# One weight stream for delta-rule inputs, queries and keys in a two-block fp32 transformer kernel, with weight units split one ahead and the modulation sums on VectorE alone

## The chip, the cores and the metric

The kernel runs on one core of a Trainium2 chip. Its metric is device time in microseconds, the median of several runs. TensorE (PE) multiplies matrices into PSUM; VectorE (DVE), ScalarE (ACT) and GpSimd (POOL) do elementwise work; SyncE (SP) here only issues DMAs. Each engine executes its own instructions in order and waits on semaphores for the others.

## The reference, cut to what matters

Two transformer blocks are applied to 256 tokens of width 2048. The first block modulates its normed input by six vectors of `c` (`w_ada`, 2048 x 12288, is the "modulation" weight), runs a latent attention (queries by `w_uq`, keys and values by `w_ukv`) beside a gated delta rule (`w_in`'s q, k, v columns pass a short convolution first), mixes both and ends with a gated feed-forward. The second has a convolution beside a windowed attention and a squared-ReLU feed-forward.

```python
mod = c_act @ w_ada[l] + b_ada[l]
sh_a, sc_a, gt_a, sh_f, sc_f, gt_f = [m[:, None, :] for m in jnp.split(mod, 6, axis=-1)]
h = _rmsnorm(x, norm_mix[l]) * (1.0 + sc_a) + sh_a
p = h @ w_in[l]
c_q, c_kv, k_pe, q_g, k_g, v_g, z, b_logit, a_logit, gate_logits = _split_cols(p)
y_a = _mla_branch(c_q, c_kv, k_pe, q_a_norm[l], kv_a_norm[l], w_uq[l], w_ukv[l], cos, sin) @ w_o_mla[l]
qkv = jnp.concatenate([q_g, k_g, v_g], axis=-1)
y_b = _gdn_branch(qkv, z, b_logit, a_logit, conv_w[l], A_log[l], dt_bias[l], gdn_norm[l]) @ w_o_gdn[l]
g_a, g_b = jnp.split(jax.nn.sigmoid(gate_logits), 2, axis=-1)
mix = (g_a * y_a + g_b * y_b) @ w_o[l]
x = x + gt_a * mix
h = _rmsnorm(x, norm_ffn[l]) * (1.0 + sc_f) + sh_f
gate, up = jnp.split(h @ w_gate_up[l], 2, axis=-1)
x = x + gt_f * ((jax.nn.silu(gate) * up) @ w_down[l])
...
def _gdn_branch(qkv, z, b_logit, a_logit, conv_w, A_log, dt_bias, gdn_norm):
    ...
    beta = jax.nn.sigmoid(b_logit.astype(jnp.float32))
    g = -jnp.exp(A_log.astype(jnp.float32)) * jax.nn.softplus(a_logit.astype(jnp.float32) + dt_bias.astype(jnp.float32))
    o = _gated_delta_chunked(q, k, v, beta, g)
```

## The kernel before

Activations lie with features on the 128 partitions and the 256 tokens along the free axis. All weights are fp32. A `Stream` reads one weight array in **units** of 128 x 1024 elements (512 KB): SP loads a unit into one of six `raw` buffers, ACT writes its rounded part `hi` (L268), DVE the remainder `lo` (L269), each into one of three buffers, and PE uses both: `mm2` (L302, L303, L305) takes a 512-column product with `hi` and a 256-column one with `lo` for each of a unit's eight blocks. So a unit costs 16 such products on PE, one ACTIVATE and one TENSOR_TENSOR. `Stream.next` hands out the blocks; when a unit is used up and none is ready it loads and splits the next one.

The stages: a first projection `wk` (96 units) with modulation vectors that PE makes itself (`ada_pe`, L426); one small product `misc`, from which the gates of the delta rule follow by a chain of small operations; then four head pairs, in which `pair_in` (convolved q, k, v by `wq`), `queries` (by `wuq` and `wuk`), `pair_mid` and `pair_out` (the delta rule) and `attend` are generators that `merge` steps in order of their costs; `wab` (output projections), `wo`, the first feed-forward (`wgu` and `wdn` in turn, three groups), the second block's `wag`, `wv2`, `wqk`, `wo2`, and its feed-forward (`wup` and `wdn2` in turn, four groups).

Beside these runs a list of fillers: at each new unit `pump` adds `rate[0]` to a credit, and each whole credit makes one step of the first filler. Twelve groups of modulation chunks (`ada_vec`, eight units each, L433 to L447) are such fillers up to `wo`, four more stand in the first feed-forward. A step of `ada_vec` loads one unit into a `raw` buffer; ACT multiplies its first half by a scalar (L440), DVE adds the second half times a scalar (L441), and POOL adds the result to the sum (L443). When a group ends, `ada_fin` (L451, L455) sums it over the partitions on PE.

A scheduler fixes each engine's order when the program is built: an instruction that was emitted earlier goes first among those that its model takes to be ready. The lines are those of the kernel before.

Of the kernel before, what the change touches and what calls it, by code (L numbers as in the profile page):

```python
# [10 lines left out]
AF = mybir.ActivationFunctionType  # L11
# [3 lines left out]
P = 128  # L15
T = 256
D = 2048
# [64 lines left out]
def layout(I):  # L82
# [34 lines left out]
    parts = [wi[:, 1024:1088], wi[:, 5184:5200], np.zeros((D, 48), np.float32)]  # L117
    for h in range(NH):
        for b in (1088, 2112, 3136):
            parts.append(wi[:, b + 128 * h:b + 128 * h + 128])  # L120
    A["wq"] = _blocks(np.concatenate(parts, 1), [(k, c) for c in range(25) for k in range(KT)])
    uq = I["w_uq"][0].reshape(512, 8, 192)
    parts = []
    for h in range(0, 8, 2):
        parts += [uq[:, h, 128:], uq[:, h + 1, 128:], uq[:, h, :128], uq[:, h + 1, :128]]
    A["wuq"] = _blocks(np.concatenate(parts, 1), [(k, c) for c in range(12) for k in range(4)])
    ukv = I["w_ukv"][0].reshape(512, 8, 2, 128)
    A["wuk"] = _blocks(ukv[:, :, 0].reshape(512, 1024), [(k, c) for c in range(8) for k in range(4)])
# [27 lines left out]
def emit(nc, tc, st, a):  # L156
# [87 lines left out]
    class Stream:  # L244
# [168 lines left out]
    def ada_pe(stream, chunks):  # L413
# [3 lines left out]
        for k in range(0, KT, 4):  # L417
            if k:
                yield
            w = []  # L420
            for g in range(4):
                if n * g % stream.size == 0:
                    w.append(stream.unit())
# [68 lines left out]
    def ada_group(ks):  # L492
# [4 lines left out]
        else:  # L497
            for k in ks[::2]:
                yield from ada_pe(ada0, [16 + k, 17 + k, k, k + 1])
# [4 lines left out]
    warm = ps("ps")  # L504
    for i in range(20):
        PE.matmul(warm[:, :P], ones, ones, start=True, stop=True)
# [12 lines left out]
    for gi, ks in enumerate(KGROUPS):  # L519
        drain()  # L520
# [3 lines left out]
        if gi + 1 < len(KGROUPS):  # L524
            nx = KGROUPS[gi + 1]
            filler.append(ada_group(nx))
# [809 lines left out]
```

## Time and profile before

| | |
|---|---|
| median of 3 runs | 2780.33 us (2779.88 to 2781.22) |
| the profiled execution: time, span | 2776.44 us, 2774.7 us |
| PE, weight loads, DVE, ACT, POOL busy | 96%, 82%, 70%, 50%, 13% of the span |
| HBM read | 563.07 MB, 205 GB/s with the writes |

The span runs from the first to the last instruction; the profiled time is 1.7 us longer. A busy PE isn't PE at its peak, so the stages are judged against the two feed-forwards, where PE never idles. PEclk is the granted clock: 1.00 is 2.4 GHz, 0.50 is 1.2 GHz.

### The profile page before, as it was taken

The page shows a single profiled execution, that of the slowest core. Times are in us where ns is not written, and L with a number is a line of the kernel's source. Part 1 is how long each engine was busy: PE and PEld are TensorE (multiplying, and loading weights), DVE is VectorE, ACT ScalarE, POOL GpSimd, SP SyncE. Part 2 cuts the span into 40 slices and gives each one's busy share as a digit, 9 for nine tenths or more (in the row PEclk, how much of TensorE's full clock was granted, in tenths as well). Part 3 has the DMA queues.
Part 4 walks back from the last instruction along what each step waited for, and adds up shares of the span by engine and source line. Part 5 has one row for each costly group of instructions (what it writes and reads, how often), then busy time and mean ns, then how long its engine had stood idle before and what let it go on. Part 6 is the DMA issues. An engine that isn't in the chain of part 4 may idle for free.

```text
span 2774.7 us, 42925 instructions
## 1 busy us (share of the span) xinstructions
PE 2677.4 (96%) x16226; PEld 2275.6 (82%) x16226; DVE 1941.0 (70%) x3066; ACT 1379.0 (50%) x2218; POOL 361.1 (13%) x310
## 2 busy tenths in 40 slices
PE   8999989899989999999999999999989999999997
PEld 5667867777777888888888889888978888888886
DVE  4865687778787877666666689796776566665665
ACT  5334565556554655344434564456554444453453
POOL 0000032223243122000000040000450000000012
PEclk9999989999999999999999999999999999999999
DMA  8795765548787687555555555544545555555553
GB/s 307 275 348 194 256 218 189 170 143 276 268 285 259 212 274 265 189 189 186 190 188 189 189 183 183 190 153 136 184 136 190 190 188 190 187 189 190 189 190 122
DMA packets 171279, 572.19 MB, mean 206 GB/s; under 512 B 19008, under 2 KB 19264, under 8 KB 171072
## 3 DMA queue, kind: packets, MB, share of 16 engines
q1 hardware_dynamic: 164736, 557.92, 59.5%
q10 hardware_dynamic: 6336, 11.53, 1.2%
q8 instruction: 128, 2.10, 0.3%
q14 instruction: 79, 0.65, 0.1%
HBM read 563.07 MB, written 6.29 MB: 205 GB/s over the span
## 4 chain that ended last, share of the span: by engine, by line
PE 78%; DVE 8%; DMA 5%; ACT 3%; issue 3%; POOL 2%; SPq 0%; ACTq 0%; DVEq 0%; POOLq 0%
PE ps L303 17%; PE ps L302 17%; PE ps L305 17%; PE ps L324 4%; PE ps L325 4%; PE ps L326 4%; PE ps L291 3%; PE ps L289 3%; PE ps L290 3%; DVE lo L269 3%; DMA raw<-ada 3%; PE O L426 1%; ACT hi L268 1%; DMA raw<-adaf 1%; DVE raw L441 1%
## 5 line engine op out<-in xcount | busy, mean ns | idle before, releaser
L269 DVE TENSOR_TENSOR lo<-raw,hi 128x1024 fp32r<-128x1024 f32 x856 | 1086.3, 1270 | 453.0 <-ACT hi L268 438.9
L268 ACT ACTIVATE hi<-raw 128x1024 fp32r<-128x1024 f32 x856 | 904.6, 1057 | 787.7 <-PE ps L305 442.1
L303 PEld LDWEIGHTS ps<-H,lo 128*128 128x128 f32 x2816 | 531.2, 189 | 139.2 <-DVE lo L269 21.8
L303 PE MATMUL ps<-H,lo 128*128 128x256 f32 x2816 | 576.5, 281 | 13.1 <-DVE lo L269 12.7
L302 PE MATMUL ps<-H,hi 128*128 128x512 f32 x1408 | 561.9, 400 | 15.5 <-DVE H L340 7.2
L305 PE MATMUL ps<-H,hi 128*128 128x512 f32 x1408 | 557.6, 397 | 0.1
L303 PEld LDWEIGHTS ps<-G,lo 128*128 128x128 f32 x1968 | 369.1, 188 | 92.1 <-DVE lo L269 7.1
L303 PE MATMUL ps<-G,lo 128*128 128x256 f32 x1968 | 389.7, 279 | 5.1 <-DVE lo L269 5.1
L305 PE MATMUL ps<-G,hi 128*128 128x512 f32 x984 | 388.7, 396 | 0.0
L302 PE MATMUL ps<-G,hi 128*128 128x512 f32 x984 | 386.9, 396 | 0.4 <-DVE Y L1056 0.4
L302 PEld LDWEIGHTS ps<-H,hi 128*128 128x128 f32 x1408 | 269.0, 191 | 22.7 <-DVE H L340 8.2
L377 POOL TENSOR_TENSOR acc<-acc,th 128x256 f32<-128x256 f32 x90 | 106.9, 1195 | 1318.4 <-ACT th L380 1317.4
L443 POOL TENSOR_TENSOR ada<-ada,raw 128x512 f32<-128x512 f32 x112 | 182.0, 1625 | 720.9 <-DVE raw L441 601.8
L305 PEld LDWEIGHTS ps<-H,hi 128*128 128x128 f32 x1408 | 265.7, 189 | 2.9 <-DVE H L340 0.3
L302 PEld LDWEIGHTS ps<-G,hi 128*128 128x128 f32 x984 | 187.0, 190 | 1.7 <-issue 0.7
L305 PEld LDWEIGHTS ps<-G,hi 128*128 128x128 f32 x984 | 184.8, 188 | 1.0
L324 PE MATMUL ps<-hi,H 128*128 128x512 f32 x448 | 175.7, 401 | 3.5 <-ACT hi L268 2.9
L325 PE MATMUL ps<-lo,H 128*128 128x512 f32 x448 | 177.0, 395 | 1.1 <-DVE lo L269 1.1
L326 PE MATMUL ps<-hi,H 128*128 128x512 f32 x448 | 175.8, 392 | 0.0
L289 PE MATMUL ps<-H,hi 128*128 128x256 f32 x528 | 151.5, 287 | 0.0
L291 PE MATMUL ps<-H,lo 128*128 128x256 f32 x528 | 151.4, 287 | 0.0
L290 PE MATMUL ps<-H,hi 128*128 128x256 f32 x528 | 151.4, 287 | 0.0
(394 smaller groups left out, 3384.5 us busy)
## 6 DMA issues: line engine op xcount, KB each, us to landing
raw<-wdn SPq DMA_DIRECT2D x216, 512.0 KB, 3.3
raw<-wgu SPq DMA_DIRECT2D x176, 512.0 KB, 3.3
raw<-wup SPq DMA_DIRECT2D x128, 512.0 KB, 3.3
raw<-wk SPq DMA_DIRECT2D x96, 512.0 KB, 5.2
raw<-ada SPq DMA_DIRECT2D x96, 512.0 KB, 4.5
raw<-wo SPq DMA_DIRECT2D x64, 512.0 KB, 4.2
Y<-ada SPq DMA_DIRECT2D x112, 256.0 KB, 5.6
raw<-wq SPq DMA_DIRECT2D x50, 512.0 KB, 4.3
```

Of the source, the lines that this page charges most:

```text
L268: S.activation(hi[:, sl], raw[:, sl], AF.Copy)
L269: V.tensor_tensor(lo[:, sl], raw[:, sl], hi[:, sl].bitcast(F32), op=ALU.subtract)
L289: PE.matmul(out, wh, x[:, HI], start=first, stop=False)
L290: PE.matmul(out, wh, x[:, LO], start=False, stop=False)
L291: PE.matmul(out, wl, x[:, HI], start=False, stop=last)
L302: PE.matmul(out, wh, x, start=first, stop=False)
L303: PE.matmul(out[:, LO], wl, x[:, HI], start=False, stop=last and wide)
L305: PE.matmul(out, wh, x, start=False, stop=last)
L324: PE.matmul(out, x[:, h], wh, start=(i == 0), stop=False)
L325: PE.matmul(out, x[:, h], wl, start=False, stop=False)
L326: PE.matmul(out, x[:, l], wh, start=False, stop=(i == n - 1))
L443: G.tensor_tensor(s, s, a0, op=ALU.add)
```

## The change

The change does five things. The arrays `wuq` and `wuk` go into `wq`, in the order of use, so that one stream feeds `pair_in` and `queries`, which are chained instead of merged. `Stream.next`, for every stream, splits the following unit as soon as it hands out the last one that is ready. `ada_vec` has no ACT and no POOL operation left: DVE does two scalar-times-tensor-plus-sum steps for each unit, and the next unit is loaded one step early. The small chain on the gates becomes a generator (`decays`) that is merged with the first pair. The fillers of the first projection stand in one list at one rate, other rates change a little, and twenty products of ones at the start are gone.

```diff
-RATE0 = (1.7, 1.3, 1.3, 1.25, 1.25)
+RATE0 = 0.85
-RATES = (0.85, 0.85, 0.62, 1.8, 1.1, 3.5, 4.2, 2.3)
+RATES = (0.8, 0.8, 0.62, 1.8, 1.3, 3.5, 4.2, 2.3)
...
+    order = [blk(heads[:, :P])]
+    for hp in range(4):
+        order.append(blk(heads[:, P + 768 * hp:P + 768 * hp + 768]))
+        h = 2 * hp
+        order.append(blk(np.concatenate([uq[:, h, 128:], uq[:, h + 1, 128:], uq[:, h, :128], ukv[:, h, 0],
+                                         uq[:, h + 1, :128], ukv[:, h + 1, 0]], 1)))
...
                 self.hi, self.lo = self.ready.pop(0)
                 self.i = 0
+                if not self.ready and self.u < self.src.shape[0]:
+                    self.ahead()
                 pump()
...
-    def ada_pe(stream, chunks):
+    def ada_pe(stream, chunks, more=False):
...
+            need = 4 * n // stream.size
+            w = [stream.unit() for _ in range(need)]
+            if k + 4 < KT or more:
+                stream.prefetch(need - len(stream.early))
...
-    def ada_vec(stream, chunks):
+    def ada_vec(stream, chunks, shared=False):
         s = tl("ada", (P, 512))
...
             w = stream.unit()
+            if stream.u < stream.src.shape[0] and k < KT - 2:
+                stream.prefetch(1)
             a0, a1 = w[:, :512], w[:, 512:]
-            S.activation(a0, a0, AF.Copy, scale=cact[:, k:k + 1])
-            V.scalar_tensor_tensor(a0 if k else s, a1, cact[:, k + 1:k + 2], a0, op0=ALU.mult, op1=ALU.add)
-            if k:
-                G.tensor_tensor(s, s, a0, op=ALU.add)
+            c0, c1 = cact[:, k:k + 1], cact[:, k + 1:k + 2]
...
+                if k:
+                    V.scalar_tensor_tensor(s, a0, c0, s, op0=ALU.mult, op1=ALU.add)
+                else:
+                    V.tensor_scalar(s, a0, c0, None, op0=ALU.mult)
+                V.scalar_tensor_tensor(s, a1, c1, s, op0=ALU.mult, op1=ALU.add)
...
-    warm = ps("ps")
-    for i in range(20):
-        PE.matmul(warm[:, :P], ones, ones, start=True, stop=True)
...
-        drain()
+        while len(h) <= ks[-1]:
+            step()
...
-        if gi + 1 < len(KGROUPS):
-            nx = KGROUPS[gi + 1]
-            filler.append(ada_group(nx))
-            rate[0] = (4 * len(nx) if nx[0] < NS else 3 * len(nx)) / (6 * len(ks)) * RATE0[gi]
+            for nx in KGROUPS[1:]:
+                filler.append(ada_group(nx))
+            rate[0] = RATE0
...
+    def decays():
+        pt = ps("ax")
...
-    merge(pair_in(0), chain(latents(), rotary_tables(), shared_key(), values(), queries(0, todo[0])))
+    merge(chain(pair_in(0), values(), queries(0, todo[0])), latents(), decays(), chain(rotary_tables(), shared_key()))
...
-    merge(pair_mid(0), pair_in(1), *[attend(*t) for t in todo[0]], queries(1, todo[1]))
-    merge(pair_mid(1), pair_out(0), pair_in(2), *[attend(*t) for t in todo[1]], queries(2, todo[2]))
-    rate[0] = RATES[1]
+    merge(pair_mid(0), chain(pair_in(1), queries(1, todo[1])), *[attend(*t) for t in todo[0]])
+    merge(pair_mid(1), pair_out(0), chain(pair_in(2), queries(2, todo[2])), *[attend(*t) for t in todo[1]])
```

Three places show what becomes of the order. The first is ACT just after `misc`, ahead of the first split of a `wq` unit after it (`Y` are the latents, `th` and `s` the convolution, `kdf` and `bef` the gates, the first `Z` the sine table). Before:

```order
L339 ACTIVATE Y_3145<-ax_3142,vec 128x256
L339 ACTIVATE Y_3157<-ax_3154,vec 128x256
L889 ACT_TABLE_LOAD
L889 ACTIVATE Z_3005<-ca_3166 128x256
L642 ACTIVATE s_3118<-up_3115,vec 128x256
L893 ACTIVATE Z_3005<-ca_3167 128x256
L646 ACT_TABLE_LOAD
L646 ACTIVATE th_3123<-s_3118 128x256
L268 ACTIVATE hi_3129<-raw_3127 128x1024
```

The same place of the changed program:

```order
L913 ACT_TABLE_LOAD
L913 ACTIVATE Z_2941<-ca_2988 128x256
L917 ACTIVATE Z_2941<-ca_2989 128x256
L670 ACT_TABLE_LOAD
L670 ACTIVATE th_3097<-s_3092 128x256
L344 ACTIVATE Y_3133<-ax_3130,vec 128x256
L636 ACTIVATE kdf<-kdf 128x16
L637 ACTIVATE bef<-bef 128x16
L271 ACTIVATE hi_3103<-raw_3101 128x1024
```

The gates `kdf` and `bef` stand behind the tables now, and one of the four table loads between `misc` and this split (that for `kdf`) is gone; the split itself still stands behind all of them.

The second place is DVE in the first feed-forward's gate and up projections, with modulation steps between them. Before:

```order
L269 TENSOR_TENSOR lo_9556<-raw_9553,hi_9555 128x1024
L1092 SCALAR_TENSOR_TENSOR tx_9538<-th_9540,tx_9538 128x256
L269 TENSOR_TENSOR lo_9583<-raw_9580,hi_9582 128x1024
L441 SCALAR_TENSOR_TENSOR raw_9635<-raw_9635,cact 128x512
L1091 TENSOR_TENSOR tx_9539<-ps_9437,tx_9539 128x256
L1093 TENSOR_TENSOR tx_9538<-tx_9538,tx_9539 128x256
L269 TENSOR_TENSOR lo_9610<-raw_9607,hi_9609 128x1024
```

In the changed program:

```order
L272 TENSOR_TENSOR lo_10072<-raw_10069,hi_10071 128x1024
L455 SCALAR_TENSOR_TENSOR ada_9846<-raw_10138,cact,ada_9846 128x512
L458 SCALAR_TENSOR_TENSOR ada_9846<-raw_10138,cact,ada_9846 128x512
L272 TENSOR_TENSOR lo_10098<-raw_10095,hi_10097 128x1024
L1111 TENSOR_TENSOR tx_10117<-ps_10019,tx_10117 128x256
L1115 SCALAR_TENSOR_TENSOR tx_10117<-th_10119,tx_10117 128x256
L272 TENSOR_TENSOR lo_10135<-raw_10132,hi_10134 128x1024
```

One scalar-times-tensor step for each modulation unit has become two, and they read the loaded `raw` unit themselves, ahead of the next `lo`.

The third place is the turn from `wgu` to `wdn` in the first feed-forward, on DVE of the changed program; raw_10551 is a `wgu` unit, raw_10596 and raw_10602 are `wdn` units:

```order
L272 TENSOR_TENSOR lo_10528<-raw_10525,hi_10527 128x1024
L272 TENSOR_TENSOR lo_10554<-raw_10551,hi_10553 128x1024
L1111 TENSOR_TENSOR tx_10573<-ps_10475,tx_10573 128x256
L1115 SCALAR_TENSOR_TENSOR tx_10573<-th_10575,tx_10573 128x256
L272 TENSOR_TENSOR lo_10599<-raw_10596,hi_10598 128x1024
L470 TENSOR_TENSOR mv<-ax_10588,vec 128x2 x2
L1114 TENSOR_TENSOR tx_10574<-ps_10476,tx_10574 128x256
L1116 TENSOR_TENSOR tx_10573<-tx_10573,tx_10574 128x256
L272 TENSOR_TENSOR lo_10605<-raw_10602,hi_10604 128x1024
```

And on PE, where that `wgu` unit is first used, right behind the last `wdn` unit of the group (`G` are the hidden activations, `H` the normed inputs):

```order
L308 MATMUL ps_11306<-G_10583,lo_11310 128x256
L310 MATMUL ps_11306<-G_10583,hi_11309 128x512
L307 MATMUL ps_11353<-H_8687,hi_10553 128x512
L308 MATMUL ps_11353<-H_8687,lo_10554 128x256
L308 MATMUL ps_11353<-H_8702,lo_10554 128x256
```

So hi_10553 and lo_10554 are made before the first `wdn` unit and lie in one of the three buffers of each kind for all 32 `wdn` units; only two are left to those. In the program before no unit is made that early.

## Rows read from the trace of the kernel before

**Rows 1.** Busy time of each engine by stage, granted clock, DMA share
```profile
core 0: us, PE busy (x) PEld busy (x) DVE busy (x) ACT busy (x) POOL busy (x), PEclk, DMA share, GB/s
12.00:23.00 11.00, 6.73 (x47) 3.49 (x48) 4.66 (x19) 2.81 (x6) 0.00 (x0) 0.73 1.04 404
...
358.00:376.00 18.00, 11.00 (x38) 7.24 (x38) 13.15 (x29) 13.19 (x23) 4.29 (x4) 0.53 0.14 42
376.00:736.00 360.00, 336.93 (x2648) 278.86 (x2647) 285.14 (x583) 209.15 (x512) 105.01 (x100) 0.98 0.61 208
736.00:850.00 114.00, 103.93 (x529) 85.80 (x528) 100.48 (x123) 62.94 (x89) 54.85 (x35) 0.97 0.84 307
...
903.00:1095.00 192.00, 186.66 (x1048) 159.29 (x1049) 157.04 (x207) 110.12 (x171) 43.45 (x28) 0.99 0.76 255
1100.00:1600.00 500.00, 500.00 (x2873) 436.23 (x2872) 308.91 (x390) 227.71 (x298) 2.31 (x2) 1.00 0.57 189
```

**Rows 2.** PE's waits, 350 to 700: us in total, times, longest
```profile
PE ps L303 <- DVE lo L269: 6.7, 9, 1.6
PE ps L302 <- ACT hi L268: 6.1, 2, 4.7
...
PE ps L291 <- DVE lo L269: 2.1, 3, 1.1
```

**Rows 3.** Instructions in time order, ACT and PE, after `misc`
```profile
368.81 1.04 ACT L268 ACTIVATE hi<-raw 128x1024 fp32r<-128x1024 f32 x1
...
369.90 0.80 PE L302 MATMUL ps<-H,hi 128*128 128x512 f32 x1 [4.72 <-ACT hi L268]
```

**Rows 4.** The split on DVE at 350, 700, 900 and 1100: busy, mean ns
```profile
L269 DVE TENSOR_TENSOR lo<-raw,hi 128x1024 fp32r<-128x1024 f32 x69 | 95.6, 1387 | 16.0 <-ACT hi L268 15.7
...
L269 DVE TENSOR_TENSOR lo<-raw,hi 128x1024 fp32r<-128x1024 f32 x59 | 82.8, 1404 | 19.6 <-ACT hi L268 18.7
...
L269 DVE TENSOR_TENSOR lo<-raw,hi 128x1024 fp32r<-128x1024 f32 x64 | 93.9, 1467 | 9.8 <-ACT hi L268 8.8
...
L269 DVE TENSOR_TENSOR lo<-raw,hi 128x1024 fp32r<-128x1024 f32 x180 | 220.6, 1225 | 128.3 <-ACT hi L268 123.3
```

**Rows 5.** Instructions in time order, POOL and DVE, first feed-forward
```profile
932.18 1.35 POOL L443 TENSOR_TENSOR ada<-ada,raw 128x512 f32<-128x512 f32 x1 [39.22 <-DVE raw L441]
...
932.30 2.31 DVE L269 TENSOR_TENSOR lo<-raw,hi 128x1024 fp32r<-128x1024 f32 x1
```

**Rows 6.** Modulation steps: POOL of all, DVE at 350, 700 and 900
```profile
L443 POOL TENSOR_TENSOR ada<-ada,raw 128x512 f32<-128x512 f32 x112 | 182.0, 1625 | 720.9 <-DVE raw L441 601.8 <-DVE ada L441 39.2 <-PE ps L324 27.2
...
L441 DVE SCALAR_TENSOR_TENSOR raw<-raw,cact 128x512 f32<-128x512 f32 x47 | 39.7, 845 | 4.7 <-ACT raw L440 4.6
...
L441 DVE SCALAR_TENSOR_TENSOR raw<-raw,cact 128x512 f32<-128x512 f32 x35 | 35.9, 1028 | 2.0 <-ACT raw L440 2.0
...
L441 DVE SCALAR_TENSOR_TENSOR raw<-raw,cact 128x512 f32<-128x512 f32 x28 | 21.1, 752 | 16.8 <-ACT raw L440 16.8
```

**Rows 7.** ACT's waits for modulation loads, from 700 and from 900
```profile
ACT raw L440 <- DMA raw<-ada: 14.3, 15, 2.0
...
ACT raw L440 <- DMA raw<-ada: 47.0, 24, 4.2
```

**Rows 8.** PE's waits over the whole span: us in total, times, longest
```profile
PE ax L451 <- POOL ada L443: 3.1, 3, 1.5
```

**Rows 9.** Unit boundaries in time order: `wdn`, then `wup`
```profile
1122.44 1.22 DVE L269 TENSOR_TENSOR lo<-raw,hi 128x1024 fp32r<-128x1024 f32 x1 [1.56 <-ACT hi L268]
...
1123.94 0.39 PE L302 MATMUL ps<-G,hi 128*128 128x512 f32 x1
...
1124.17 0.40 PE L303 MATMUL ps<-G,lo 128*128 128x256 f32 x2
...
2306.51 0.39 ACT L1293 ACTIVATE tx<-ps 128x256 f32<-128x256 f32 x1 [1.68 <-PE ps L305]
...
2306.79 1.05 ACT L268 ACTIVATE hi<-raw 128x1024 fp32r<-128x1024 f32 x1
```

More of the change, by code (lines that the diff above doesn't have):

```diff
@@ L568, in emit @@
     S.activation(misc, pm, AF.Copy)
-    pt = ps("ax")
-    for j in range(2):
-        PE.transpose(pt[:, P * j:P * j + P], misc[:, P * j:P * j + P], ident)
     lg = one("lg", (P, 2, 16))
-    V.tensor_copy(lg, pt.rearrange("p (j c) -> p j c", j=2)[:, :, 64:80])
     beta, g, ab, nb, ex, u, ln = [one(n, (P, 2, 8)) for n in ("beta", "g", "ab", "nb", "ex", "u", "ln")]
-    S.activation(beta, lg[:, :, 0:8], AF.Tanh, scale=0.5)
-    V.tensor_scalar(beta, beta, 0.5, 0.5, op0=ALU.mult, op1=ALU.add)
@@ new lines, in decays @@
+    def decays():
+        pt = ps("ax")
+        for j in range(2):
+            PE.transpose(pt[:, P * j:P * j + P], misc[:, P * j:P * j + P], ident)
+        V.tensor_copy(lg, pt.rearrange("p (j c) -> p j c", j=2)[:, :, 64:80])
+        S.activation(beta, lg[:, :, 0:8], AF.Tanh, scale=0.5)
+        yield 1.5
+        V.tensor_scalar(beta, beta, 0.5, 0.5, op0=ALU.mult, op1=ALU.add)
+        V.tensor_tensor(g, lg[:, :, 8:16], vc("dt", 0, 8)[:, None, :].to_broadcast([P, 2, 8]), op=ALU.add)
+        V.tensor_scalar(nb, g, -1.0, None, op0=ALU.mult)
+        V.tensor_tensor(ab, g, nb, op=ALU.max)
+        S.activation(ex, ab, AF.Exp, scale=-1.0)
+        yield 1.5
+        V.tensor_scalar(u, ex, 1.0, None, op0=ALU.add)
+        S.activation(ln, u, AF.Ln)
+        yield 1.5
+        V.scalar_tensor_tensor(nb, u, -1.0, ex, op0=ALU.add, op1=ALU.subtract)
+        V.reciprocal(ab, u)
+        V.tensor_tensor(nb, nb, ab, op=ALU.mult)
+        V.tensor_tensor(ln, ln, nb, op=ALU.subtract)
+        yield 1.5
+        V.scalar_tensor_tensor(g, g, 0.0, ln, op0=ALU.max, op1=ALU.add)
+        ea = sm(8)
+        S.activation(ea, vc("alog", 0, 8), AF.Exp)
+        yield 1.5
+        V.tensor_scalar(ea, ea, -1.0, None, op0=ALU.mult)
+        V.tensor_tensor(g, g, ea[:, None, :].to_broadcast([P, 2, 8]), op=ALU.mult)
+        pg = ps("ax")
+        yield 1.5
+        PE.matmul(pg[:, 0:16], cn["trib"], f16(g), start=True, stop=True)
+        PE.matmul(pg[:, 16:32], ones[LOW], f16(g)[LOW], start=True, stop=True)
+        pg2 = ps("ax")
+        PE.matmul(pg2[:, 0:16], ones[HIGH], f16(g)[HIGH], start=True, stop=True, tile_position=(64, 0))
+        yield 1.5
+        V.tensor_copy(f16(cum), pg[:, 0:16])
+        V.tensor_copy(f16(tot0), pg[:, 16:32])
+        V.tensor_tensor(f16(kdf), pg2[:, 0:16], f16(cum), op=ALU.subtract)
+        V.tensor_tensor(kdf[LOW], tot0[LOW], kdf[LOW], op=ALU.add)
+        V.tensor_tensor(cumt[LOW], cum[LOW], tot0[LOW], op=ALU.subtract)
+        V.tensor_copy(cumt[HIGH], cum[HIGH])
+        yield 1.5
+        V.tensor_copy(bef[LOW], cum[LOW])
+        V.tensor_tensor(bef[HIGH], cum[HIGH], tot0[HIGH], op=ALU.add)
+        V.tensor_scalar(nfull, bef, -1.0, None, op0=ALU.mult)
+        S.activation(kdf, kdf, AF.Exp)
+        S.activation(bef, bef, AF.Exp)
+        yield 1.5
+        V.tensor_tensor(bef, bef, beta, op=ALU.mult)
+        V.tensor_scalar(ncum, cum, -1.0, None, op0=ALU.mult)
+        V.tensor_scalar(hb, beta, 0.5, None, op0=ALU.mult)
+        yield 1.0
@@ L909, in shared_key @@
         yield 1.0
-    wuv, wuq, wuk = Stream("wuv", 512), Stream("wuq"), Stream("wuk")
+    wuv = Stream("wuv", 512)
     vt = [None, None]
@@ L959, in queries @@
         p = ps("ps")
-        yield from proj_g(p, wuq, lat[0])
+        yield from proj_g(p, wq, lat[0])
         t, qp = tl("ca"), tl("qk")
@@ L965, in queries @@
             p = ps("ps")
-            yield from proj_g(p, wuq, lat[0])
+            yield from proj_g(p, wq, lat[0])
             qn = tl("s2")
@@ L969, in queries @@
             p = ps("ps")
-            yield from proj_g(p, wuk, lat[1])
+            yield from proj_g(p, wq, lat[1])
             kn = tl("s2")
@@ L1074, in emit @@
     for q in range(12, 16):
-        filler.append(ada_vec(ada1, [32 + 4 * q + i for i in range(4)]))
+        filler.append(ada_vec(ada1, [32 + 4 * q + i for i in range(4)], False))
     rate[0] = RATES[2]
```

62 lines of the change are left out of this document (13 added, 49 removed).

## The prediction

> **What bounds the kernel now.** I read the busy time by stage first. In the first feed-forward, 1100 to 1600, PE is busy for all 500 us at a granted clock of 1.00, that is 2.4 GHz: 2873 products in 500 us, 16 to a unit, make 2.78 us for a unit [rows 1]. Nothing can be won there except by less work on PE, and the change takes none away. What can be won lies between 344 and 1100, where PE is not full: 23.1 us idle of the 360 from 376 to 736 (360 less 336.93), 10.1 from 736 to 850, 5.3 from 903 to 1095, and the 18 us from 358 to 376, in which PE is busy for 11.0 at a mean clock of 0.53, so nearly all of it at 1.2 GHz [rows 1]. In the same table DVE is the engine to watch: 100.5 of 114 us (88%) from 736 to 850, 79% from 376 to 736, 82% from 903 to 1095, while ACT is at 55 to 58% in these.
>
> The waits of PE come next. From 350 to 700 it waits 6.7 us for `lo`, 6.1 for `hi` and 2.1 for `lo` in another form of product, 14.9 us together [rows 2]. One of these waits is 4.72 us, at 369.90 [rows 3]: the `hi` that PE lacks starts on ACT at 368.81, after a row of table loads and small copies that stand ahead of it. The others are ten or more and short.
>
> The last view groups the split on DVE by stage: the same 128x1024 subtraction takes 1225 ns where POOL is idle, and 1387, 1404 and 1467 on average in the three stages where POOL adds up the modulation sums [rows 4]. In time order the cause is plain: a `lo` that overlaps one of POOL's adds takes 2.31 us [rows 5]. So today each modulation unit costs DVE its own step (845, 1028 and 752 ns in the three stages [rows 6]) and part of a blocked one besides.
>
> **The change part by part.** The sum is made against the profiled execution's own time, 2776.4 us; the median of the runs shown is 3.9 above it, and I add that at the end.
>
> *After `misc`.* With a unit split one ahead, the order has one more unit of `wq` ready ahead of the ACT row that holds up PE. The late split itself still stands behind the tables. At 1.2 GHz one more unit is worth twice 2.78 us, so 5.6 us of the wait are covered. The bounds: nothing, if the stall only moves one unit on; and 12 us, if the 11.0 busy us ran at full clock without waits (11.0 x 0.53 = 5.8 of 18). I take -5.6.
>
> *One stream in the pair merges.* Before, `pair_in` runs beside `queries`, so that `wq`, `wuq` and `wuk` can each hold a partly used unit, and there are three buffers of `hi` and `lo`: the next unit can't be split until one is used up. After, there is one stream with one unit in use and one ready. Of the 14.9 us of split waits 10.2 remain without the 4.7 above; the mean clock of 0.98 over 360 us costs 7.2 more [rows 1, 2]. Bounds: 0 and 17.4. I take half, -8.7, because PE's other idle time here (23.1 less 10.2) waits for the delta rule's own chain, which stays. DVE's load hardly speaks against it: the order has 112 steps instead of 61 between the 96th and the 176th unit, at 0.75 us instead of 0.845 that is 84.0 instead of 51.5, less 80 splits that are 0.162 us shorter (13.0): 19.5 more in about 390 us, and 79% become some 84%.
>
> *The sums without POOL.* PE waits 3.1 us for POOL's last adds, in 3 places [rows 8]. DVE takes POOL's place there without a hand-over: between 0 and -3.1, I take -2.0.
>
> *From 736 to 850.* Between the 176th and the 212th unit the order has 79 modulation steps on DVE where there were 35 (the rate goes from 1.1 to 1.3). 79 at 0.752, as in the stage where they were least disturbed, are 59.4; 35 at 1.028 were 36.0 [rows 6]. So DVE gains 23.4, and loses 36 x (1.404 - 1.225) = 6.4 by undisturbed splits [rows 4]: 100.5 + 17.0 = 117.5 us of work in a stage that lasts 114. If DVE never idled the stage would grow by 3.5; with the 13.5 us that it idles today, by 17. A bound engine idles less, so I stay near the lower end: +5.0.
>
> How much POOL's adds cost DVE matters here. By rows the three stages' splits lose 69 x 0.162 + 59 x 0.179 + 64 x 0.242 = 37 us [rows 4]. The Trainium skill, page "SBUF — State Buffer", section "Who interferes with whom", says that a DVE instruction with two SBUF inputs contends with a GpSimd instruction that reads SBUF, and that the loser fully blocks; by that alone up to POOL's whole 182.0 us [rows 6] would come back to DVE, and the terms for its load would turn into gains. The averages are far from that (I suppose that most adds fall beside instructions that are not stopped), and I go by them.
>
> *From 903 to 1095.* DVE gets 64 steps for 32, 24 us more, and 66 splits that are 0.242 us shorter, 16 less: 165 of 192, still covered by PE's 187. ACT's 47.0 us of waits for modulation loads, with the next `hi` queued behind them, go away [rows 7]; the loads are issued a step earlier, but what waits for them now is DVE. PE idles 5.3 here: between 0 and -5.3, I take -2.0.
>
> *One split unit parked.* `wgu` and `wdn`, `wup` and `wdn2` alternate. By splitting ahead, the stream that pauses keeps a unit in one of the three buffers, so a `hi` can start only when PE has finished the unit before last, one unit of PE time (2.78 us) ahead of its use instead of two. The rows show how well that fits: `lo` starts at 1122.44, ends at 1123.66, and the product at the same place of the next unit, 1124.17, is 0.51 later [rows 9]. Where ScalarE copies an output first, `hi` starts 0.28 later [rows 9], which leaves 0.23. About 367 units run like this, 76 of them behind such a copy (28 in gate and up, 48 in `wup`). Nothing is lost by the rows; if each of the 76 lost its 0.28, it would be 21 us. I take +2.0.
>
> *The rest.* The twenty products at the start are no loss: the clock falls to a mean of 0.73 from 12 to 23 in spite of them [rows 1], and PE waits for loads there, the DMA share being 1.04; if all its 6.73 busy us ran at 1.2 GHz it would be 3.1 us, and I take 0. The first projection's fillers keep their work, and PE is the bound there: 0.
>
> Sum: -5.6 - 8.7 - 2.0 + 5.0 - 2.0 + 2.0 = -11.3; 2776.4 - 11.3 + 3.9 = 2769.0.
>
> **The rivals.** (1) *Nothing comes of it*: the split waits are the delta rule's chain in another form, and what PE no longer waits for `lo` it waits for the chain. For it: after the split waits 13 us of idle time stay from 376 to 736. Time: 2780.
>
> (2) *DVE is held up by loads*, and the kernel gets slower. ACT waited 14.3 us from 700 to 900 and 47.0 from 900 to 1100 for modulation loads [rows 7]; now DVE would stand there, with the splits behind it. From 736 to 850 it has no slack, so the 14.3 would come through whole; from 903 to 1095 it has 192 - 165 = 27 free, and 20 would. -11.3 + 34 + 2780.3 = 2803. It decides once DVE's waits for `raw` pass 27 us in the second stage. Against it: the load is one step earlier. The Trainium skill, page "Perfetto Trace Analysis", section "Identifying the Most-Contended Engine", takes VectorE's occupancy as a fair measure of how close it is to its limit; by that rule 88% before and over 100% of the stage's old length after make DVE the bound from 736 to 850, and moving work onto it is wrong there.
>
> (3) *The parked unit costs*: 21 us instead of 2 give 2769 + 19 = 2788. It decides if a `hi` or `lo` is late by more than 0.23 to 0.51 us at unit boundaries. Against it: the rows leave that margin.
>
> (4) *All waits go*: 12 + 23.1 + 3.1 + 5.3 = 43.5 less the 7.0 of the two losses give 2744. For it: ACT loses its modulation steps, and POOL no longer disturbs DVE.
>
> **How the numbers follow.** A measurement of this kernel can tell about 0.2%, 5.6 us, from no change. My forecast, 2757 to 2774, has 0.47; (1) 0.20; (2) 0.15; (3) 0.10; (4) 0.08. So faster 0.55, same 0.20, slower 0.25. The range, 2750 to 2792, takes in the forecast, (1) and (3), and leaves out most of (2) and (4).
>
> **What would show it.** After `misc`, PE's wait for `hi` should fall below 2 us and the time at 1.2 GHz should shrink; the waits for `lo` and `hi` up to 700 should be about half of 14.9; the split should take 1.23 us everywhere; DVE should be over 95% busy in the output projections; PE should stay full in both feed-forwards, with 2.78 us for a unit. I would be wrong if DVE waits long for `raw`, if units in the feed-forwards take 2.8 us or more, or if the delta rule's own waits grow by what the splits lose.

## The result and the profile after

The changed kernel takes 2745.39 us (2742.74 to 2748.43, 4 runs) against 2780.11 of the kernel before on the same chip; the ratio is 0.9881 (95% interval 0.9859 to 0.9903). So it is 34.7 us faster: the direction was forecast, the size is three times the forecast's 11.3, and the time lies below the range. The profiled execution took 2743.0 us, its span is 2741.2.

Busy time by stage, with the stretches laid so that they answer to [rows 1]:

```profile
core 0: us, PE busy (x) PEld busy (x) DVE busy (x) ACT busy (x) POOL busy (x), PEclk, DMA share, GB/s
12.00:23.00 11.00, 7.89 (x44) 3.96 (x38) 3.56 (x17) 2.17 (x5) 0.00 (x0) 1.00 1.04 410
357.00:375.00 18.00, 10.96 (x48) 8.04 (x48) 14.64 (x46) 11.02 (x20) 1.53 (x3) 0.72 0.19 63
375.00:705.00 330.00, 325.42 (x2624) 270.73 (x2624) 289.02 (x630) 174.70 (x454) 29.69 (x49) 1.00 0.65 221
705.00:819.00 114.00, 101.43 (x501) 79.83 (x500) 106.92 (x157) 39.88 (x54) 6.58 (x6) 0.99 0.88 310
877.00:1069.00 192.00, 191.68 (x1098) 167.14 (x1098) 160.73 (x247) 95.22 (x144) 0.00 (x0) 0.99 0.79 265
1100.00:1600.00 500.00, 500.00 (x2872) 435.93 (x2871) 316.02 (x404) 237.42 (x322) 19.82 (x18) 1.00 0.57 189
```

In the head pairs PE had 2648 products in 360 us, now 2624 in 330; its idle time there went from 23.1 us to 4.6 and its mean clock from 0.98 to 1.00, and of the 30 us the idle time is 18.5. In the start of the feed-forward it has 1098 products in 192 us where it had 1048. The output projections (705 to 819) aren't better, and the steady feed-forward is the same.

PE's waits from 348 to 700 (us in total, times, longest), which answer to [rows 2]:

```profile
PE ps L307 <- ACT hi L271: 3.2, 1, 3.2
PE ax L619 <- DVE g L615: 1.8, 1, 1.8
...
PE ps L330 <- DVE lo L272: 1.1, 2, 0.8
```

Most of the waits for splits are gone. With one more row for `lo` (0.7) they are 5.0 us; before, [rows 2] give 14.9, and 16.0 with a row of 1.1 for `hi` that they don't show. The long one, 3.25 us instead of 4.72, stands behind the tables as in [rows 3], and now behind the gates `kdf` and `bef` too, for which ACT itself waits for DVE:

```profile
362.57 1.28 ACT L670 ACT_TABLE_LOAD   x1
...
365.75 0.22 ACT L636 ACTIVATE kdf<-kdf 128x16 f32<-128x16 f32 x1 [1.10 <-DVE kdf L628]
...
367.21 0.21 ACT L637 ACTIVATE bef<-bef 128x16 f32<-128x16 f32 x1 [1.24 <-DVE ab L635]
...
367.33 1.99 ACT L271 ACTIVATE hi<-raw 128x1024 fp32r<-128x1024 f32 x2
...
368.42 0.80 PE L307 MATMUL ps<-H,hi 128*128 128x512 f32 x1 [3.25 <-ACT hi L271]
```

DVE's groups from 348 to 700 (count, then busy and mean ns of one, then idle time before them), answering to [rows 4] and [rows 6]:

```profile
L272 DVE TENSOR_TENSOR lo<-raw,hi 128x1024 fp32r<-128x1024 f32 x77 | 94.5, 1232 | 9.0 <-ACT hi L271 8.9
L458 DVE SCALAR_TENSOR_TENSOR ada<-raw,cact,ada 128x512 f32<-128x512 f32 x54 | 41.2, 764 | 0.4
L455 DVE SCALAR_TENSOR_TENSOR ada<-raw,cact,ada 128x512 f32<-128x512 f32 x47 | 36.7, 781 | 0.2
L668 DVE SCALAR_TENSOR_TENSOR s<-up,vec,s 128x256 f32<-128x256 f32 x72 | 35.0, 486 | 0.0
```

The split takes 1232 ns where it took 1387, and the convolution's 72 steps (last row) 486; before the change they took 560, which the prediction had not looked at:

```profile
L644 DVE SCALAR_TENSOR_TENSOR s<-up,vec,s 128x256 f32<-128x256 f32 x72 | 40.3, 560 | 3.1 <-ACT s L642 2.6
```

For the rest I cut every trace into stages at the first product of each on PE, which the time order gives; in the changed kernel these are:

```profile
342.73 0.28 PE L294 MATMUL ps<-H,hi 128*128 128x256 f32 x1
...
705.46 0.39 PE L329 MATMUL ps<-hi,Y 128*128 128x512 f32 x1
...
761.04 0.74 PE L307 MATMUL ps<-G,hi 128*128 128x512 f32 x2 [0.59 <-ACT hi L271]
...
875.97 0.77 PE L307 MATMUL ps<-H,hi 128*128 128x512 f32 x1 [1.73 <-DVE sm L496]
...
1061.36 0.47 PE L307 MATMUL ps<-G,hi 128*128 128x512 f32 x1
```

The lengths between such places in each profiled execution (us; the experiments are told below):

| kernel | to `misc` | `misc` and pairs | `wab` with yb | `wo` | gate and up, first group | rest | span |
|---|---|---|---|---|---|---|---|
| before | 343.8 | 392.4 | 56.8 | 109.9 | 193.1 | 1678.7 | 2774.7 |
| changed | 342.7 | 362.7 | 55.6 | 114.9 | 185.4 | 1679.8 | 2741.2 |
| no split ahead | 346.0 | 369.0 | 60.3 | 117.1 | 185.1 | 1677.3 | 2754.7 |
| and three streams | 345.3 | 378.1 | 58.5 | 118.0 | 184.5 | 1677.8 | 2762.1 |
| sums on three engines | 343.2 | 380.3 | 56.6 | 117.7 | 193.6 | 1677.7 | 2769.2 |
| before, sums on DVE | 346.1 | 380.6 | 55.3 | 111.3 | 184.0 | 1677.5 | 2754.9 |
| ACT's multiply | 342.6 | 366.7 | 55.1 | 113.5 | 184.2 | 1679.2 | 2741.2 |
| and short idle additions | 342.6 | 371.7 | 57.4 | 112.6 | 191.8 | 1678.8 | 2754.9 |
| three engines, short additions | 343.2 | 367.5 | 51.9 | 107.5 | 185.0 | 1680.4 | 2735.6 |
| the same, no additions | 342.3 | 358.7 | 48.9 | 107.5 | 184.9 | 1678.2 | 2720.4 |

So 29.7 us came in the stage with the pairs and 7.7 in the first gate and up group; `wo` gave 5.0 back.

### The profile page after: what moved, and what is told of

Same layout as the page of the kernel before. It is cut to its first block, busy times and chain, and to the rows that moved or that the text cites. A ratio compares the mean times of both kernels' runs of the same rounds, so it can differ in the third digit from the quotient of the medians.

```text
span 2741.2 us, 42462 instructions
## 1 busy us (share of the span) xinstructions
PE 2662.6 (97%) x16186; PEld 2263.6 (83%) x16186; DVE 1955.0 (71%) x3194; ACT 1299.4 (47%) x2089; POOL 179.1 (7%) x198
## 3 DMA queue, kind: packets, MB, share of 16 engines
q1 hardware_dynamic: 164736, 557.92, 60.3%
## 4 chain that ended last, share of the span: by engine, by line
PE 69%; DVE 5%; issue 1%; POOL 1%; ACT 1%; DMA 1%; POOLq 0%; ACTq 0%; DVEq 0%
PE ps L310 18%; PE ps L307 18%; PE ps L308 18%; PE ps L294 3%; PE ps L296 3%; PE ps L295 3%; DVE lo L272 2%; PE ps L330 1%; PE ps L331 1%; PE ps L329 1%; DVE Y L1152 1%; DVE ada L458 1%; DVE ada L455 1%; PE ax L1234 1%; PE O L1252 0%
## 5 line engine op out<-in xcount | busy, mean ns | idle before, releaser
L272 DVE TENSOR_TENSOR lo<-raw,hi 128x1024 fp32r<-128x1024 f32 x856 | 1048.0, 1226 | 457.9 <-ACT hi L271 446.9
L310 PEld LDWEIGHTS ps<-G,hi 128*128 128x128 f32 x984 | 185.0, 188 | 1.1
L329 PEld LDWEIGHTS ps<-hi,H 128*128 128x128 f32 x448 | 83.7, 189 | 47.2 <-issue 18.9
```

The lines of the kernel that those rows point to most:

```text
L272: V.tensor_tensor(lo[:, sl], raw[:, sl], hi[:, sl].bitcast(F32), op=ALU.subtract)
L310: PE.matmul(out, wh, x, start=False, stop=last)
L329: PE.matmul(out, x[:, h], wh, start=(i == 0), stop=False)
```

## The experiments

My theory after the comparison was that the order of the splits had given the 30 us of the pairs (A); the rival, that ACT and POOL are free of the sums (B). Medians are given. A ratio's interval is about 0.0016 to either side, 4.5 us, so differences of a few us between two kernels are not settled by them. The scheduler orders every kernel anew, so most of these kernels differ from each other in order as well as in the edit; two comparisons below don't.

**No split ahead.** The changed kernel without

```diff
-                if not self.ready and self.u < self.src.shape[0]:
-                    self.ahead()
```

> The changed kernel, but a unit is split only when the one before it is used up, as before the change. Where the change gained 34.7 us by the medians, some 30 of them in the four head pairs (386.4 us from the small product to the end of the last pair before, 356.7 after) and some 7 in the start of the first feed-forward. Theory A, the order of the splits (one stream, one unit split ahead): this takes at least half of the 30 away, so 2760 us or more, with the waits of PE for hi and lo up to 700 back at 10 us or more from 5. Theory B, the engines of the sums (ACT and POOL free of them, splits undisturbed): the pairs stay within 5 us of 357, the time is 2750 or less. A parked unit that cost something in the feed-forwards would show as units shorter than in the changed kernel; I expect 2.78 us in both.

2754.97 us, 0.9919 (0.9904 to 0.9934). The pairs lose 6.3 us of the 29.7, neither theory's number, and the waits for `hi` and `lo` from 348 to 705 are 5.0 us still, not 10. So the split ahead is a part of it, not the bulk. It also helps ahead of `misc` (3.3 us) and in `wab` (4.7).

**Three streams again, no split ahead.**

```diff
-    merge(pair_mid(0), chain(pair_in(1), queries(1, todo[1])), *[attend(*t) for t in todo[0]])
+    merge(pair_mid(0), pair_in(1), *[attend(*t) for t in todo[0]], queries(1, todo[1]))
...
-    wuv = Stream("wuv", 512)
+    wuv, wuq, wuk = Stream("wuv", 512), Stream("wuq"), Stream("wuk")
```

> The changed kernel without the unit split ahead and with three streams again for the delta rule's inputs, queries and keys, merged as before; the sums stay on VectorE alone and the gates stay a generator. Theory A (order): the pairs are back at 380 us or more, the total at 2768 or more. Theory B (engines of the sums): the pairs stay near 360, the total at 2752 or less. If the one stream matters apart from the split ahead, this is longer than the run without the split ahead by what it is worth.

2763.27 us, 0.9955 (0.9939 to 0.9971), with 378.1 us for the pairs: 9.1 more than with one stream. Half of the gain in the pairs is the order, half is something else.

**Sums on three engines, and the sums alone.** The first puts ACT, DVE and POOL back into the changed kernel, the second puts the new `ada_vec` alone into the kernel before.

```diff
-    def ada_vec(stream, chunks, shared=False):
+    def ada_vec(stream, chunks, shared=True):
```

> The changed kernel, but each modulation unit is summed on ACT, DVE and POOL again (the early load stays). Theory A (order): it loses only the 7 us of the first feed-forward's start and some 2 for PE's waits on POOL, so about 2754, with the pairs within 5 us of 357. Theory B (engines of the sums): the pairs are back at 380 us or more, the total at 2770 or more. Either way the split beside POOL should be back at about 1.39 to 1.47 us on average.

> The kernel before, with one part of the change: the modulation sums on VectorE alone, the next unit loaded a step early. Theory A (order): the pairs stay near 386, the start of the first feed-forward gains 7 us, the total is about 2770. Theory B (engines of the sums): the pairs fall to 362 or less, the total to 2752 or less. A third way, that neither part does it alone, would leave this at 2770 or more and also cost the run with the sums on three engines 20 us or more.

The first takes 2773.76 us, 0.999 (0.998 to 1.0001): without the new sums the rest of the change is worth little. The second takes 2757.58, 0.9928 (0.9912 to 0.9945): the sums alone give 20.5 us. Of the stage with the pairs the table makes a square: the sums give 11.8 us in the old order and 17.6 in the new one; the order gives 12.1 with the old sums and 17.9 with the new. The gate and up group belongs to the sums alone (184.0, 185.4 with them, 193.1, 193.6 without). "Order" here is all the rest of the change, the gates' generator and the rates among it, which I did not part in this stage. PE's idle time from 32 us after `misc` to the end of the pairs says the same: 23.1 us before, 17.0 with the order alone, 14.5 with the sums alone, 4.6 with both. Both theories are half right, and the one that the prediction had priced at next to nothing, the sums, is the larger in the total.

**Which engine?** Two kernels separate ACT's share from POOL's. In the first ACT multiplies again and DVE adds; in the second DVE does both steps and POOL adds beside them, with a result that nobody reads.

```diff
+            S.activation(a0, a0, AF.Copy, scale=c0)
+            V.scalar_tensor_tensor(a0 if k else s, a1, c1, a0, op0=ALU.mult, op1=ALU.add)
+            if k:
+                V.tensor_tensor(s, s, a0, op=ALU.add)
...
+            V.scalar_tensor_tensor(s, a1, c1, s, op0=ALU.mult, op1=ALU.add)
+            if k:
+                G.tensor_tensor(a0, a1, s, op=ALU.add)
```

> The changed kernel, but ACT multiplies the first half of each modulation unit again, and DVE does the step of before plus POOL's addition; POOL has none of it. The run with the sums on three engines lost 28.4 us, 17.6 of them from the small product to the end of the pairs and 8.2 in the start of the first feed-forward. Theory C, ACT's share and its waits for the modulation loads with the next hi behind them: this run loses most of the 28, so 2760 us or more. Theory D, POOL's adds beside DVE's work: it loses less than 8, so 2753 or less, and the split stays at 1.23 us.

> The changed kernel, with one addition on POOL after each modulation step, of the same size and shape as the one of before, whose result nobody reads; DVE's two steps stay, ACT's share stays off. Theory D (POOL's adds beside DVE): the splits take 1.35 us or more on average, the pairs grow by 10 us or more, the start of the first feed-forward by 8, the total is 2760 or more. Theory C (ACT's share): 2750 or less, though the splits are longer. If both this run and the one with ACT's multiply stay under 2750, it takes both together.

With ACT's multiply it is 2739.84 us, 0.987 (0.9855 to 0.9885): no cost of ACT's share shows. With POOL's additions it is 2828.5, 1.0186 (1.0171 to 1.0201), the slowest of all. It is POOL's addition; but that kernel overstates it, since the addition reads the sum that DVE writes next, and DVE waits for it (350 to 1069, first row of DVE's waits):

```profile
DVE ada L449 <- POOL raw L454: 43.2, 41, 1.5
```

**What of POOL?** Three kernels with ACT's multiply and work on POOL that nobody waits for, inside the raw unit after DVE has read it: an addition of 512 columns, one of 16, and three fills of 512.

```diff
                 V.tensor_tensor(s, s, a0, op=ALU.add)
+                G.tensor_tensor(a0, a0, a1, op=ALU.add)
...
+                G.tensor_tensor(a0[:, :16], a0[:, :16], a1[:, :16], op=ALU.add)
...
+                for _ in range(3):
+                    G.memset(a0, 0.0)
```

> The run with ACT's multiply (2739.84 us), with a POOL addition of the old size after each modulation step, inside the raw unit, after DVE has read it: nobody waits for its result, only the unit's buffer comes free later. The first run with a POOL addition beside took 2828.5 us, but there DVE waited over 40 us for POOL, since the addition read the sum that DVE writes next. Theory D (the additions stretch DVE's instructions with both inputs in SBUF): the pairs grow by 10 us or more from 366.7, the start of the first feed-forward by 5 or more from 184.2, the splits take 1.33 us or more and the convolution's steps 0.55 or more in place of 0.48; total 2760 or more. Theory E (the later release of the buffer, or the waits of PE and DVE for POOL's sums, cost it): under 2748, since nobody waits for sums here.

> The same with an addition of 16 columns instead of 512: POOL still has the buffer last and starts at the same places, but for a short time. Theory D: within 4 us of the run with ACT's multiply, 2740 to 2745, splits at 1.23 us. Theory E (the release through POOL costs it): as long as the run with the full additions.

> The same with three fills of 512 columns on POOL, about 1.6 us for each modulation step, in place of the addition: POOL is as busy, and the buffer is free as late, but POOL reads nothing. If it is POOL's reading that stretches DVE's instructions, the splits stay at 1.23 us and the total within 5 us of the run with the short additions; if it is any POOL work, the splits take 1.33 us or more and the total is near that of the full additions. The Trainium skill, page 'SBUF — State Buffer', section 'Who interferes with whom', says that a DVE instruction with two SBUF inputs contends with a GpSimd instruction that reads SBUF and not with one that only writes it; by that this run stays short.

The full addition takes 2819.75 us (1.0147, 1.0132 to 1.0163), the short one 2758.76 (0.9928, 0.9913 to 0.9942), the fills 2754.28 (0.9915, 0.9898 to 0.9931). The split from 350 to 1069 in these three, in this order, and POOL's work in the first and the third:

```profile
L272 DVE TENSOR_TENSOR lo<-raw,hi 128x1024 fp32r<-128x1024 f32 x170 | 234.5, 1381 | 26.4 <-ACT hi L271 25.3
...
L272 DVE TENSOR_TENSOR lo<-raw,hi 128x1024 fp32r<-128x1024 f32 x188 | 230.3, 1227 | 35.0 <-ACT hi L271 33.8
...
L272 DVE TENSOR_TENSOR lo<-raw,hi 128x1024 fp32r<-128x1024 f32 x189 | 230.6, 1223 | 35.3 <-ACT hi L271 33.9
...
L452 POOL TENSOR_TENSOR raw<-raw 128x512 f32<-128x512 f32 x101 | 178.2, 1767 | 350.7 <-DVE ada L451 193.2 <-issue 62.7 <-ACT G L344 38.7
...
L453 POOL MEMSET raw<- 128x512 f32 x333 | 174.5, 527 | 366.6 <-DVE ada L451 249.8 <-ACT G L344 39.1 <-ACT hi L271 34.5
```

POOL is busy for as long with the fills as with the full additions, so it is POOL's reading that stretches DVE, not its being busy. The Trainium skill, page "SBUF — State Buffer", section "Who interferes with whom", says that a DVE instruction with two SBUF inputs contends with a GpSimd instruction that reads SBUF and not with one that only writes it. The trace agrees: the split takes 1381 ns on average in the run with the full additions and 1223 in the one with the fills, where the 94 splits that run beside a fill take 1219. Over the whole span DVE is busy for 2016.6 us with the full additions and 1942.5 with the fills, and between these kernels, which also differ in order, 74.1 us of it come with 65.5 of time. But the short addition and the fills, which stretch next to nothing (DVE is busy for 1939.4 and 1942.5 us, 1938.9 without work on POOL), still cost 18.9 and 14.4 us: I had expected the former within 4. So there is a second way. I take it to be the late release of the buffer: the kernel with the short addition has the load queue and, but for a few places, PE, DVE and ACT in the same order as the one without, and DVE is as busy; what is left of its edit is when POOL lets the buffer go. The kernel with the fills has another order, so for its 14.4 us that is argued, not shown.

**Both ways in place.** The kernel with the sums on three engines, with POOL's addition cut to 16 columns, and without it; both leave most of the sums out.

```diff
-                    G.tensor_tensor(s, s, a0, op=ALU.add)
+                    G.tensor_tensor(s[:, :16], s[:, :16], a0[:, :16], op=ALU.add)
```

> The kernel with the sums on three engines (2773.76 us), with POOL's addition cut to the first 16 of 512 columns; the rest of the modulation sums is left out. DVE, ACT and the loads do what they did, and the raw buffer still comes free only after POOL. If the stretch of DVE's instructions is the larger part of the 28.4 us that this kernel loses against the changed one, this run takes 2757 or less; if the late release is the larger part, 2762 or more. From the runs with additions that nobody waits for, the release cost 18.9 us (2739.84 to 2758.76), which leaves 9.5 for the stretch: 2764.

> The same with POOL's addition left out altogether (the sums are left out but for their first step): DVE has one step for each modulation unit, and the raw buffer comes free when DVE has read it. Against the run with 16 columns this is the release alone. Release the larger part: 2748 or less, 15 us or more under that run. Stretch the larger part: within 8 us of it. DVE has half of the changed kernel's modulation work, so it can also be under 2745.

They take 2732.01 us (0.9835, 0.9819 to 0.9851) and 2722.57 (0.9809, 0.9794 to 0.9823). Shortening the addition is worth 41.8 us, far more than the 9.5 that I had left for it; taking it away another 9.4, between the 8 and the 15 that I had named as signs of the one way and of the other. In the first two of these kernels ACT and the load queue execute the same instructions in the same order, and PE and DVE but for 14 of 16186 and 2 of 3066 places, so the 41.8 us are not the work of another order. DVE's groups from 350 to 1069 show the stretch; first with the sums on three engines,

```profile
L272 DVE TENSOR_TENSOR lo<-raw,hi 128x1024 fp32r<-128x1024 f32 x183 | 256.1, 1401 | 40.8 <-ACT hi L271 39.1
L450 DVE SCALAR_TENSOR_TENSOR raw<-raw,cact 128x512 f32<-128x512 f32 x108 | 94.7, 882 | 17.4 <-ACT raw L449 17.2
L668 DVE SCALAR_TENSOR_TENSOR s<-up,vec,s 128x256 f32<-128x256 f32 x72 | 48.2, 670 | 3.1 <-ACT s L666 2.4
...
L664 DVE TENSOR_TENSOR up<-ps,th 128x256 f32<-128x256 f32 x24 | 10.0, 418 | 3.3 <-ACT th L661 3.3
```

then with the addition of 16 columns:

```profile
L272 DVE TENSOR_TENSOR lo<-raw,hi 128x1024 fp32r<-128x1024 f32 x195 | 238.5, 1224 | 60.6 <-ACT hi L271 58.1
L450 DVE SCALAR_TENSOR_TENSOR raw<-raw,cact 128x512 f32<-128x512 f32 x111 | 84.4, 766 | 26.8 <-ACT raw L449 26.5
L668 DVE SCALAR_TENSOR_TENSOR s<-up,vec,s 128x256 f32<-128x256 f32 x72 | 36.0, 500 | 2.7 <-ACT s L666 1.9
...
L664 DVE TENSOR_TENSOR up<-ps,th 128x256 f32<-128x256 f32 x24 | 10.1, 419 | 6.0 <-ACT th L661 6.0
```

The three large groups with both inputs in SBUF are shorter, by 13 to 25%; the last row, whose first input is in PSUM, is not. Start and end of each instruction show the overlap itself: with the sums on three engines 76 splits run beside one of POOL's additions for the sums and take 1663 ns on average, the other 780 take 1226; of the convolution's steps 24 run beside one and take 1008, the others 500; of the last row's, 10 take 420 beside one, the others 417. Over the whole span DVE's busy time by the pages is 1943.9 us, 1875.1 with the short addition, 1876.4 without any, and 1955.0 in the changed kernel (1941.0 before); the pages of these four, in this order:

```profile
PE 2667.4 (96%) x16186; PEld 2266.1 (82%) x16186; DVE 1943.9 (70%) x3066; ACT 1377.6 (50%) x2217; POOL 365.0 (13%) x310
```

```profile
PE 2662.1 (97%) x16186; PEld 2267.0 (83%) x16186; DVE 1875.1 (69%) x3066; ACT 1379.1 (50%) x2217; POOL 236.1 (9%) x310
```

```profile
PE 2652.7 (98%) x16186; PEld 2260.8 (83%) x16186; DVE 1876.4 (69%) x3066; ACT 1379.4 (51%) x2217; POOL 178.0 (7%) x198
```

```profile
PE 2662.6 (97%) x16186; PEld 2263.6 (83%) x16186; DVE 1955.0 (71%) x3194; ACT 1299.4 (47%) x2089; POOL 179.1 (7%) x198
```

The other way is seen on SP's queue. In the kernel before, from 903 to 1095, its longest waits in total were for POOL to release a raw buffer:

```profile
SPq L257 <- POOL ada L443: 66.5, 28, 3.5
SPq L257 <- DVE lo L269: 43.7, 22, 12.2
```

From 877 to 1069 of the changed kernel it is DVE that releases them, and the waits for a modulation unit's buffer are shorter, 1.2 us on average for 2.4:

```profile
SPq L260 <- DVE lo L272: 61.8, 30, 12.2
SPq L260 <- DVE ada L458: 29.1, 24, 2.4
```

That wait alone isn't the price. With the sums on three engines and short additions SP still waits for POOL in this stretch,

```profile
SPq L260 <- POOL ada L452: 38.5, 28, 3.5
```

and yet the stage lasts 185.0 us, 184.9 without the additions; in the run with ACT's multiply and the short addition that nobody needs, where SP waits 71.0 us for POOL, it lasts 191.8, 184.2 without that addition. What the release costs depends on what else stands in the stage.

**The rate in the output projections, and split ahead for one stream alone.**

```diff
-RATES = (0.8, 0.8, 0.62, 1.8, 1.3, 3.5, 4.2, 2.3)
+RATES = (0.8, 0.8, 0.62, 1.8, 1.1, 3.5, 4.2, 2.3)
...
-                if not self.ready and self.u < self.src.shape[0]:
+                if self.one and not self.ready and self.u < self.src.shape[0]:
```

> The changed kernel with the rate of the fillers in the output projections at 1.1 again instead of 1.3. From the start of wo to the first feed-forward, the kernels with 1.3 took 114.9 to 118.0 us, those with 1.1 took 109.9 and 111.3. If DVE's or the loads' density there costs the 5 us, this stage takes 111 or less and the total is 2740 to 2742; if the order of the pairs costs it, the stage stays at 115 and the total at 2745. Steps not made there are made in the rest of the fillers, before the feed-forward or by the drain ahead of it, and could cost as much.

> The changed kernel with the next unit split ahead in the one stream of the pairs alone; the other streams split as before, so that no unit of one stream lies in a buffer while another stream runs. If a parked unit costs something, the two feed-forwards get shorter, by up to the 21 us that I allowed for; from the first wdn unit to the end the changed kernel took 1679.8 us, the run without any split ahead 1677.3, so I expect 2 us here. If the split ahead helps in the first projection, wab and wo as well, this loses 3 us before the small product and 5 to 7 from 705 to 876. So 2745 plus or minus 8; the pairs should stay at 363.

With the old rate 2739.2 us (0.9862, 0.9845 to 0.9878): `wab` and `wo` take 53.0 and 113.7 us, 166.7 together as before the change, where the changed kernel takes 170.5. The rate fits as the cause of those 3.8, but by 2.6 in `wab` and 1.2 in `wo`, not by the 4 in `wo` that I expected. With the split ahead in `wq` alone (`self.one` is true for that stream only) it is 2751.77 (0.991, 0.9895 to 0.9925), with 364.3 us for the pairs and 1677.5 from the first `wdn` unit on against 1679.8: a parked unit costs 2.3 us by these two profiles (the kernel with the sums on three engines, which parks one too, takes 1677.7, so it isn't settled), and what the split ahead gives before the pairs and in `wab` is worth more.

**Toward a better version.** The old rate, and the split ahead everywhere but in the feed-forwards; then other rates as well.

```diff
+            self.one = name not in ("wgu", "wdn", "wup", "wdn2")
...
-RATES = (0.8, 0.8, 0.62, 1.8, 1.1, 3.5, 4.2, 2.3)
+RATES = (0.85, 0.85, 0.62, 1.8, 1.0, 3.5, 4.2, 2.3)
```

> A version for the best time: the changed kernel with the rate in the output projections at 1.1 (2739.2 us by itself) and without the unit split ahead in the feed-forward streams, where from the first wdn unit to the end the changed kernel took 1679.8 us and the one with the split ahead in the pairs alone 1677.5. If both hold and add up, 2737 us, 0.9855 of before; if the 2 us at the end are chance, 2739.

> The version for the best time (2736.47 us) with the fillers a little faster in the four head pairs (0.85 in place of 0.8) and slower in the output projections (1.0 in place of 1.1). The pairs have DMA to spare (share 0.62 against 0.86), so the output projections should lose 2 us; DVE is at 87% in the pairs, and they may gain as much. 2733 to 2740.

2736.47 us (0.9849, 0.9832 to 0.9867) and 2741.27 (0.9869, 0.9854 to 0.9884). The first is the fastest kernel here that computes all; its interval overlaps that of the changed kernel, so that it beats it isn't settled. The second lies a little above the range that I gave it: it gains 2.8 us in `wo` and loses 2.2 in the pairs.

## Why the prediction was right or wrong

*The order of the pairs: right in sum.* The terms after `misc` (-5.6) and for one stream (-8.7) are -14.3 together; measured are -12.1 with the old sums and -17.9 with the new. With the old sums the order takes PE's idle time from 23.1 to 17.0 us and its mean clock from 0.98 to 0.99, which are the two parts that the prediction halved. How the terms divide is less good. In the 32.19 us after `misc` PE had 125 products, now 146, at 0.126 us each (330.54 / 2628) 2.6 us won, and the wait for `hi` is 3.25, not under 2: I had seen only the tables ahead of that split, and the change put the gates there too, with 2.3 us of waits for DVE's chain.

*The sums without POOL, -2.0: this is the step that failed.* I gave it the 3.1 us that PE waited for POOL's last adds [rows 8]. They gave 20.5 alone and 28.4 on top of the order (some 8 to 9 of either in the stage from 903 to 1095, which had a term of its own). The last is a sum of three: the stretch gives back 41.8 (2773.76 to 2732.01), the release 9.4 (to 2722.57), and DVE's second step in place of ACT's multiply costs 22.8 (to 2745.39), or 17.3 with that multiply kept (to 2739.84). By the ratios, each against the kernel before on its own chip, the three are 43, 7 and 20 us, each uncertain by 5 to 7. The first includes that a short addition also releases the buffer sooner; the fills held it about as long as the full additions and cost no more than the short ones, which speaks against that being much of it, but that kernel has another order, and the two are not parted.

Two things went wrong in it. The stretch was sized from the splits alone, 37 us [rows 4]; the modulation steps and the convolution are stretched too, and DVE's busy time falls by 68.8 once the additions are short. And I set the stretch off against DVE's new steps, us for us, as load. They aren't alike: 68.8 us of stretch cost 41.8 us of time, 78.6 us of new steps (1876.4 to 1955.0) only 22.8. A plausible reason, not tested, is that a stretch falls on whatever DVE is doing, the splits and the delta rule's chain as well, while most modulation steps find a place where nothing waits for them.

So the sentence that PE's other idle time in the pairs "waits for the delta rule's own chain, which stays" was wrong: of 13 us most went, as 4.6 us is all the idle time that is left. Neither part did it alone (17.0 and 14.5 us); with the new order, cutting POOL's additions to 16 columns takes the 17.0 to 7.3, so most of it then hung on these additions.

*903 to 1095, -2.0:* measured -7.7, the direction right. It goes with the sums and not with the order. I looked at ACT's waits for the loads [rows 7] and not at what PE itself waited for there,

```profile
PE ps L303 <- DVE lo L269: 5.3, 9, 1.3
```

which is gone in the changed kernel, and also with short additions on POOL. That PE's idle time fell from 5.3 to 0.3 is the bound that I gave; in the rest PE's busy time for a product fell from 178 ns (186.66 / 1048) to 175 (191.68 / 1098).

*736 to 850, +5.0:* measured +3.8 over `wab` and `wo` (166.7 to 170.5), and nothing at the old rate. DVE is 94% busy there, over 95% was forecast.

*The parked unit, +2.0:* measured 1.1 us against before, 2.3 against the kernels without it; units in the steady feed-forward stay at 2.78 us. *The first projection, 0:* -1.1, and 346.0 instead of 342.7 us without the split ahead, which the term had left out. *The warm-up, 0:* the clock from 12 to 23 is 1.00 without it.

*The rivals.* From 877 to 1069 DVE waits for modulation loads less than the 27 us from which rival (2) decides:

```profile
DVE ada L455 <- DMA raw<-ada: 9.0, 11, 1.9
```

So it fell. The Trainium skill, page "Perfetto Trace Analysis", section "Identifying the Most-Contended Engine", calls the occupancy of VectorE a fair measure of how close it is to its limit. Over the whole span that misleads here: DVE is 70% busy with the sums on three engines and 71% with all of them on DVE, which is 28.4 us faster. In the output projections alone, at 94%, the new rate did cost its 3.8 us, and at the old rate the stages took 166.7 us as before. Rival (4), all waits go, came to 2744 and had 0.08. Its argument, that POOL no longer disturbs DVE, is the one that held; that its number is met to 2 us is luck, since not all waits went (PE's idle time in the pairs is 4.6 us, and the wait after `misc` 3.25).

## What to carry to other kernels

Where GpSimd and VectorE work side by side, compare the mean of every VectorE group with both inputs in SBUF, not of one, between a stage with GpSimd's work and one without; the difference is time on whatever chain VectorE serves, and it can pay to give VectorE that work outright. Here added steps cost less than the same time added to instructions that others wait for, so the two are not to be set off against each other, us for us. Read the load queue's own waits too: who releases a buffer last decides when the next load in that queue can start.

## What the runs showed of the hardware

An addition on POOL lengthens DVE's instructions with two inputs in SBUF (the split 1224 to 1401 ns on average, the convolution's step 500 to 670) and leaves one with an input in PSUM alone (419 and 418); fills on POOL, 333 of 527 ns, leave the split at 1223. It goes both ways by this profile, whose spans on POOL are rough: an addition of 16 columns takes 520 ns on average in one kernel and 768 in another, but 226 and 243 where no DVE instruction with two inputs in SBUF overlaps it, and 735 and 921 where one does. So part of the late release is the same contention. 111 of these additions, of no use but to hand a buffer back, cost 9.4 and 18.9 us.
